# One core, a hybrid transformer block in split fp32r: a fourth Strassen pair in every FFN block, low halves of one K pair by ScalarE and an accumulating DMA, one Strassen pair fewer in the down projection, and the transposed mixer output in two tiles

## The chip, the core and the metric

The kernel runs on one core of a Trainium2 chip. The metric is the device time in microseconds (us) of one execution. TensorE (PE) multiplies, VectorE (DVE), ScalarE (ACT) and GpSimd (POOL) work beside it, and SyncE (SP) and POOL issue the DMAs.

## The reference, cut to what matters

The reference is one pre-norm block over 256 tokens of width 2048, in float32:

```
u = rms_norm(h, norm_mix)
z = u @ w_in                       # 2048 x 13060: inputs of four branches, 4*2048 merge gates
branches = (diff_attention, rg_lru, forgetting_attention, sliding_window_sink_attention)
gates = sigmoid(gz + b_gate)
mixed = sum(gates[n] * (branches[n] @ w_branch[n]) for n in range(4))
h = h + mixed @ w_out
v = rms_norm(h, norm_ffn)
h = h + (silu(v @ w_ffn_gate) * (v @ w_ffn_up)) @ w_ffn_down      # width 5632
out = rms_norm(h, norm_final)
```

## The kernel before

**Splitting.** PE multiplies in fp32r. So that nothing is lost, every fp32 operand is the sum of a high part (the value rounded to fp32r) and a low part (the value less the high part), and every product is three matmuls: high by high, high by low, low by high. A weight piece comes by DMA from SP into a tile `raw` (128 x 1024, two blocks of 128 rows); `wpiece` (L118) makes the high part `whi` by a copy on ACT and the low part `wlo` by a subtraction on DVE. `raw`, `whi` and `wlo` have four buffers each, which the pieces take in turn.

**Pairs.** `pair` (L245) computes two products of 512 columns side by side, a left and a right weight, for both halves t of the tokens (128 each) and both column halves i. It walks K in steps of 256 rows, called K pairs, numbered kp. An ordinary kp takes two pieces (left, right) and 2 x 2 x 2 x 3 = 24 matmuls into the accumulators `q[t][i]`. A Strassen kp (one in `skps`) goes by seven products in place of eight, so 21 matmuls; `s_weights` (L220) prepares it: two DMAs into `sx`, four DVE additions into `sx` and `se`, two ACT copies to the high parts `sh` (128 x 2048) and `seh` (128 x 1536), and two DVE subtractions to the low parts `sl` and `sel`. In the FFN and the down projection `sx`, `sh`, `sl`, `seh`, `sel` have two buffers, `se` has one. Four of the seven products gather in banks p1, p5, p6, p7, which DVE adds up in a tile `u` when the last Strassen kp is done. The last kp's products are held back to the end (`split`).

**Stages.** First come the branches, and then four gated chunks by `chunk` (L140), up to about 384 us. Six gated pairs follow to about 705 us (L803), each with a gate pair over eight kp and a branch pair over two. Their sums `mixed_of[c]` are four tiles of 512 columns. The first two are complete early: `nat_out` (L312) transposes them on PE and POOL writes them to four DRAM tiles `mrg`, at about 500 us. Then comes the output projection (L870), two pairs over eight kp with the transposed `mixed` as left operand, in one tile for the high and one for the low parts, `mth` and `mtl`. Its K blocks 0 to 7 come back from `mrg` by four DMAs of SP (`mload`, in a buffer of pool `fp`) and are split by ACT and DVE (`m_split`, L853); its K blocks 8 to 15 are transposed straight from `mixed_of[2]` and `mixed_of[3]` (`to_T`). The FFN (L894) has eleven blocks f of 512 hidden columns, each one pair over eight kp: gate weight left, up weight right. Block 0 has no Strassen kp, odd blocks have kp 0, 2, 3 and 5, even blocks kp 0, 3 and 5. The down projection (L944) has two pairs (cc 0 and 1) over 22 kp, Strassen at kp 3, 6, 9, 12, 15 and 18. Its left operand, the hidden layer, comes from DRAM (`hid`) into slices of `fin`; ACT and DVE split it into `ah`, and a Strassen kp needs four more small additions and a split on it (`s_sums`, L199).

**Order.** The program is built by a scheduler that sets the order of the instructions on each engine by itself. On the chip each engine takes its instructions as they stand and waits for semaphores. What the scheduler made of the code is therefore shown below by the instructions as they stand, beside the diff.

Of the kernel before, what the change touches and what calls it, by code (L numbers as in the profile page):

```python
# [8 lines left out]
F32 = mybir.dt.float32  # L9
# [5 lines left out]
P = 128  # L15
# [14 lines left out]
def hybrid_block_kernel(  # L30
# [47 lines left out]
    def rd(t):  # L78
        return t.bitcast(F32)
# [35 lines left out]
        tt(o, acc, t, ALU.mult)  # L115


    def wpiece(src, nk, n, pin=False):  # L118
        raw = wp.tile([P, nk, n], F32, tag="raw", name="raw", bufs=4)
        nc.sync.dma_start(raw, src.rearrange("(k p) n -> p k n", p=P))  # L120
        hi = wp.tile([P, nk, n], F32R, tag="whi", name="whi")
        lo = wp.tile([P, nk, n], F32R, tag="wlo", name="wlo")
        ins = (act(hi, raw), tt(lo, raw, rd(hi), ALU.subtract))
        if pin:
            for i in ins:
                tc.keep_in_program_order(i)
        return hi, lo
# [114 lines left out]
        while later:  # L242
            later.pop(0)()

    def pair(wl, wr, nkp, skps, a_of, upool=None, split=0, small_banks=False, at_mid=None):  # L245

# [22 lines left out]
        for kp in range(nkp):  # L271
# [3 lines left out]
            if kp in skps:  # L275
# [8 lines left out]
                if kp == skps[-1]:  # L284
# [8 lines left out]
                    run_later()  # L293
                continue
            rows = slice(kp * 2 * P, (kp + 1) * 2 * P)
            ws = [wpiece(w[rows, :], 2, 512) for w in (wl, wr)]
            todo = [((t, i), [(blk(j, t), (ws[i][0][:, j, :], ws[i][1][:, j, :])) for j in range(2)])
                    for t in range(2) for i in range(2)]
            if kp >= nkp - split:
                held.append(todo)  # L300
                continue
# [501 lines left out]
    for n, cc in ((2, 0), (0, 0), (1, 1), (3, 1), (2, 1), (0, 1)):  # L803
# [1 line left out]
        bb = mp.tile([P, 1024], F32, tag="bb2", name="bb2")  # L805
        nc.gpsimd.dma_start(bb, b_gate[0, col:col + 1024].partition_broadcast(P))
        col += C_GZ
        q, gate = pair(w_in[:, col:col + 512], w_in[:, col + 512:col + 1024], NKT // 2, GS, u_of, mp)
        for t in range(2):
            g = gate[:, 2 * t:2 * t + 2, :]  # L810
            tt(g, g, q[t], ALU.add)
# [27 lines left out]
    s3 = ExitStack()  # L839
    mxp = s3.enter_context(tc.tile_pool(name="mxp", bufs=1, side="right"))  # L840
    late["sx"] = mxp
    mth = mxp.tile([P, NKT, S], F32R, name="mth")
    mtl = mxp.tile([P, NKT, S], F32R, name="mtl")
    vth = uv.tile([P, NKT, S], F32R, tag="th", name="vth")
    vtl = uv.tile([P, NKT, S], F32R, tag="tl", name="vtl")
    ss2 = small.tile([P, 2, 2], F32, name="ss2", bufs=1)
    m_of = a_tiles(mth, mtl)


    for c in (2, 3):  # L850
        later.append(lambda c=c: to_T(mixed_of[c], mth, mtl, 4 * c))

    def m_split(kp, s):  # L853
        if kp > 3:
            return m_of(kp, s)
        if kp % 2 == 0:
            late["m"] = fp.tile([P, 2, 512], F32, tag="hd", name="mload")
        v = late["m"][:, kp % 2, :]
        nc.sync.dma_start(v, merged[kp])
        h, lo = (t[:, 2 * kp:2 * kp + 2, :].rearrange("p a b -> p (a b)") for t in (mth, mtl))  # L860
        act(h, v)
        tt(lo, v, rd(h), ALU.subtract)
        return m_of(kp, s)
# [29 lines left out]
    v_of = a_tiles(vth, vtl, FS, vsh, vsl)  # L893
    for f in range(DFF // 512):  # L894
        fs = slice(f * 512, (f + 1) * 512)
        q, u = pair(w_fg[:, fs], w_fu[:, fs], NKT // 2, () if f == 0 else FS if f % 2 else (0, 3, 5), v_of, fp, split=1)
        hd = fp.tile([P, 2, 512], F32, tag="hd", name="hd")

        if u is None:
            for t in range(2):  # L900
                act(hd[:, t, :], q[t][:, 0, :], AF.Silu, scale=rstd2[:, t:t + 1])
                tt(hd[:, t, :], hd[:, t, :], q[t][:, 1, :], ALU.mult)
        else:
            for t in range(2):
                o = u[:, 2 * t:2 * t + 2, :]
                tt(o, o, q[t], ALU.add)
                act(u[:, 2 * t, :], u[:, 2 * t, :], AF.Silu, scale=rstd2[:, t:t + 1])
            tt(hd, u[:, 0:4:2, :], u[:, 1:4:2, :], ALU.mult)
        later.append(lambda hd=hd, f=f: nat_out(hd, hid, f"hid{f}_"))
# [7 lines left out]
    nc.gpsimd.dma_start(gfin, norm_final.partition_broadcast(P))  # L917
    ss3 = small.tile([P, 2, 3], F32, name="ss3", bufs=1)
    ah = uv.tile([P, 4, 2, 2 * S], F32R, tag="tl", name="ah")
    DS = (3, 6, 9, 12, 15, 18)  # L920

    def h_of(cc, kp, with_sums):
        if cc == 0 and kp < 4:
# [91 lines left out]
```

## Time and profile before

| | |
|---|---|
| median of three runs | 1532.04 us (1528.97 to 1533.72) |
| the profiled execution | 1530.98 us, of it the span 1529.3 us |
| PE busy | 1497.3 us, 98% of the span |
| DVE, ACT, POOL busy | 78%, 53%, 5% |
| moved by DMA | 311.5 MB |

The span is the time from the first to the last instruction; 1.7 us of the profiled execution lie around it. The profile tells for each engine how long it was busy, and the trace gives every instruction with its start, its length and the idle time of the engine before it, with what ended this idle time. Matmuls overlap: each is listed with about 0.39 us, and the step from one start to the next is what it costs. The share of busy time is a mean over stages with different limits, so the stages are read one by one.

### The profile page before, as it was taken

What the parts mean: (1) busy time and instruction counts of PE and PEld (TensorE: products, weight loads), DVE (VectorE), ACT (ScalarE), POOL (GpSimd) and SP (SyncE); (2) the same over time, 40 slices, a digit from 0 to 9 for tenths busy, and PEclk for the clock granted to TensorE, in tenths of its full rate; (3) what the DMA queues carried; (4) which work ended last, traced back from release to release, by engine and by line L of the source; (5) the groups of instructions that cost most, each with busy time, mean ns of one, the idle gap of its engine ahead of it and who ended that gap; (6) DMA issues with size and microseconds to landing.
All of it is one profiled execution on the core that took longest, in us unless ns stands there. A gap on an engine that the chain in (4) does not pass through costs nothing.

```text
span 1529.3 us, 18519 instructions
## 1 busy us (share of the span) xinstructions
PE 1497.3 (98%) x6772; PEld 1230.8 (80%) x6772; DVE 1191.7 (78%) x1397; ACT 817.0 (53%) x944; POOL 74.4 (5%) x95
## 2 busy tenths in 40 slices
PE   8999999999999999998999999999999999999997
PEld 6878888888788888886888888888888888877875
DVE  4756745769779779866467899999999898899785
ACT  5545744545445544534356555555555565665553
POOL 4000300011100000000000000000000000001001
PEclk9999999999999999998999999999999999999999
DMA  7755465567566667565657666666756668776753
GB/s 231 214 146 166 136 182 153 170 186 247 179 207 218 222 207 218 181 192 193 192 178 237 220 220 221 203 234 205 233 176 233 191 223 302 241 235 215 237 178 125
DMA packets 158603, 311.54 MB, mean 204 GB/s; under 512 B 10608, under 2 KB 12720, under 8 KB 158384
## 3 DMA queue, kind: packets, MB, share of 16 engines
q1 hardware_dynamic: 154528, 297.87, 61.9%
q0 software_dynamic: 3952, 12.49, 2.6%
q8 instruction: 53, 0.87, 0.2%
q14 instruction: 38, 0.31, 0.1%
q10 hardware_dynamic: 32, 0.01, 0.0%
HBM read 301.41 MB, written 8.91 MB: 203 GB/s over the span
## 4 chain that ended last, share of the span: by engine, by line
PE 90%; DVE 4%; DMA 3%; issue 2%; ACT 0%; POOL 0%; SPq 0%; POOLq 0%; ACTq 0%; DVEq 0%
PE q L216 52%; PE acc L133 20%; PE p L216 14%; PE ps L165 2%; DMA fin<-hid 1%; DVE wlo L60 1%; DMA mload<-mrg 1%; DMA xq<-in_x_dram 1%; DVE sel L60 1%; DVE ah L60 0%; DVE se L60 0%; DMA raw<-in_w_in_dram 0%; PE ps L535 0%; PE ps L731 0%; PE ps L554 0%
## 5 line engine op out<-in xcount | busy, mean ns | idle before, releaser
L57 ACT ACTIVATE whi<-raw 128x1024 fp32r<-128x1024 f32 (+1 forms) x418 | 437.7, 1050 | 420.2 <-PE q L216 189.5
L60 DVE TENSOR_TENSOR wlo<-raw,whi 128x1024 fp32r<-128x1024 f32 (+1 forms) x418 | 509.0, 1224 | 190.4 <-ACT whi L57 187.5
L57 ACT ACTIVATE sh<-sx 128x2048 fp32r<-128x2048 f32 x59 | 113.0, 1916 | 120.7 <-issue 38.5
L133 PE MATMUL acc<-wlo,uth 128*128 128x512 f32 (+1 forms) x448 | 173.9, 391 | 0.0
L133 PE MATMUL acc<-whi,utl 128*128 128x512 f32 (+1 forms) x448 | 173.7, 389 | 0.0
L60 DVE TENSOR_TENSOR sl<-sx,sh 128x2048 fp32r<-128x2048 f32 x59 | 135.1, 2289 | 44.3 <-ACT sh L57 44.2
L133 PE MATMUL acc<-whi,uth 128*128 128x512 f32 (+1 forms) x448 | 167.9, 391 | 0.6 <-DVE nat L64 0.4
L216 PE MATMUL q<-wlo,vth 128*128 128x512 f32 x424 | 165.8, 391 | 0.0
L216 PE MATMUL q<-whi,vtl 128*128 128x512 f32 x424 | 165.6, 391 | 0.0
L216 PE MATMUL q<-whi,vth 128*128 128x512 f32 x424 | 164.5, 391 | 0.0
L216 PE MATMUL q<-whi,ah 128*128 128x512 f32 x480 | 151.4, 392 | 0.0
L216 PE MATMUL q<-whi,uth 128*128 128x512 f32 x288 | 111.0, 391 | 2.4 <-DVE gate L60 2.4
L216 PE MATMUL q<-wlo,uth 128*128 128x512 f32 x288 | 111.6, 390 | 0.0
L216 PE MATMUL q<-whi,utl 128*128 128x512 f32 x288 | 111.5, 390 | 0.0
L216 PEld LDWEIGHTS q<-whi,ah 128*128 128x128 f32 x480 | 90.8, 189 | 18.9
L60 DVE TENSOR_TENSOR sel<-se,seh 128x1536 fp32r<-128x1536 f32 x59 | 103.3, 1751 | 2.3 <-ACT seh L57 2.3
L216 PE MATMUL q<-wlo,ah 128*128 128x512 f32 x240 | 94.9, 395 | 4.9 <-DVE wlo L60 4.8
L133 PEld LDWEIGHTS acc<-wlo,uth 128*128 128x128 f32 x448 | 84.8, 189 | 17.0 <-issue 1.0
L133 PEld LDWEIGHTS acc<-whi,utl 128*128 128x128 f32 x448 | 84.8, 189 | 16.4 <-issue 0.7
L133 PEld LDWEIGHTS acc<-whi,uth 128*128 128x128 f32 x448 | 82.1, 189 | 16.9 <-issue 0.7
L57 ACT ACTIVATE seh<-se 128x1536 fp32r<-128x1536 f32 x59 | 87.2, 1479 | 15.7 <-DVE se L60 8.5
L216 PEld LDWEIGHTS q<-whi,vth 128*128 128x128 f32 x424 | 79.6, 188 | 16.3
(388 smaller groups left out, 2520.5 us busy)
## 6 DMA issues: line engine op xcount, KB each, us to landing
raw<-in_w_in_dram SPq DMA_DIRECT2D x168, 512.0 KB, 3.7
raw<-in_w_ffn_down_dram SPq DMA_DIRECT2D x64, 512.0 KB, 5.2
raw<-in_w_ffn_gate_dram SPq DMA_DIRECT2D x53, 512.0 KB, 4.2
raw<-in_w_ffn_up_dram SPq DMA_DIRECT2D x53, 512.0 KB, 4.8
sx<-in_w_ffn_up_dram SPq DMA_DIRECT2D x35, 512.0 KB, 3.8
sx<-in_w_ffn_gate_dram SPq DMA_DIRECT2D x35, 512.0 KB, 4.8
raw<-in_w_branch_dram SPq DMA_DIRECT2D x32, 512.0 KB, 4.4
raw<-in_w_out_dram SPq DMA_DIRECT2D x32, 512.0 KB, 4.5
```

Of the source, the lines that this page charges most:

```text
L57: return nc.scalar.activation(o, i, f, **kw)
L60: return (eng or nc.vector).tensor_tensor(out=o, in0=a, in1=b, op=op)
L133: m = nc.tensor.matmul(acc, x_, w_, start=st, stop=sp_)
L165: nc.tensor.transpose(pt[:, i * S + t * P:i * S + (t + 1) * P], nat[:, t, (c0 + i) * P:(c0 + i + 1) * P], ident)
L216: m = nc.tensor.matmul(acc, x_, w_, start=st, stop=sp_)
```

## The change

Five edits. (1) In `pair`, `swap` lets kp 0 begin with the token half t = 1; it is set for the first of the six gated pairs. (2) `mth` and `mtl` become two tiles each, one for K blocks 0 to 7 (`mh0`, `ml0`) and one for K blocks 8 to 15 (`mh1`, `ml1`), and `mload` takes the buffer `gate` of pool `gp`. (3) In FFN blocks 1 to 10 both pieces of kp 6 get their low part in another way: ACT writes the negated, rounded weight into `wlo`, and POOL issues a DMA that adds the weight from DRAM onto it; ACT makes `whi` as before. (4) FFN blocks 2, 4, 6, 8 and 10 get the fourth Strassen kp, 2. (5) In the down projection kp 18 becomes an ordinary one in both pairs.

```
-    def wpiece(src, nk, n, pin=False):
+    def wpiece(src, nk, n, pin=False, by_dma=False):
         raw = wp.tile([P, nk, n], F32, tag="raw", name="raw", bufs=4)
         nc.sync.dma_start(raw, src.rearrange("(k p) n -> p k n", p=P))
         hi = wp.tile([P, nk, n], F32R, tag="whi", name="whi")
         lo = wp.tile([P, nk, n], F32R, tag="wlo", name="wlo")
+        if by_dma:
+            act(lo, raw, scale=-1.0)
+            nc.gpsimd.dma_start(lo, src.rearrange("(k p) n -> p k n", p=P), accum_op=ALU.add)
+            act(hi, raw)
+            return hi, lo
...
-            ws = [wpiece(w[rows, :], 2, 512) for w in (wl, wr)]
+            ws = [wpiece(w[rows, :], 2, 512, by_dma=kp in dma_kps) for w in (wl, wr)]
             todo = [((t, i), [(blk(j, t), (ws[i][0][:, j, :], ws[i][1][:, j, :])) for j in range(2)])
-                    for t in range(2) for i in range(2)]
+                    for t in ((1, 0) if swap and kp == 0 else (0, 1)) for i in range(2)]
...
-        q, gate = pair(w_in[:, col:col + 512], w_in[:, col + 512:col + 1024], NKT // 2, GS, u_of, mp)
+        q, gate = pair(w_in[:, col:col + 512], w_in[:, col + 512:col + 1024], NKT // 2, GS, u_of, mp,
+                       swap=(n, cc) == (2, 0))
...
-    mth = mxp.tile([P, NKT, S], F32R, name="mth")
-    mtl = mxp.tile([P, NKT, S], F32R, name="mtl")
+    mt = [[mxp.tile([P, NKT // 2, S], F32R, name=f"m{hl}{half}") for hl in "hl"] for half in (1, 0)][::-1]
...
-    m_of = a_tiles(mth, mtl)
+    def m_of(kp, s):
+        return a_tiles(*mt[kp // 4])(kp % 4, s)
...
-        later.append(lambda c=c: to_T(mixed_of[c], mth, mtl, 4 * c))
+        later.append(lambda c=c: to_T(mixed_of[c], mt[1][0], mt[1][1], 4 * (c - 2)))
...
-            late["m"] = fp.tile([P, 2, 512], F32, tag="hd", name="mload")
+            late["m"] = gp.tile([P, 2, 512], F32, tag="gate", name="mload")
         v = late["m"][:, kp % 2, :]
         nc.sync.dma_start(v, merged[kp])
-        h, lo = (t[:, 2 * kp:2 * kp + 2, :].rearrange("p a b -> p (a b)") for t in (mth, mtl))
+        h, lo = (t[:, 2 * kp:2 * kp + 2, :].rearrange("p a b -> p (a b)") for t in mt[0])
...
-        q, u = pair(w_fg[:, fs], w_fu[:, fs], NKT // 2, () if f == 0 else FS if f % 2 else (0, 3, 5), v_of, fp, split=1)
+        q, u = pair(w_fg[:, fs], w_fu[:, fs], NKT // 2, () if f == 0 else FS, v_of, fp, split=1,
+                    dma_kps=() if f == 0 else (6,))
...
-    DS = (3, 6, 9, 12, 15, 18)
+    DS = (3, 6, 9, 12, 15)
```

The scheduler builds another order from this. ACT in FFN block 5, before: `sh_8244` and `seh_8246` are kp 3's, `whi_8373` and `whi_8379` kp 6's, `sh_8317` and `seh_8319` kp 5's, and `u` is the block before's.

```order
L57 ACTIVATE u_8025<-u_8025,rstd2_6471 128x512 x2
L57 ACTIVATE sh_8244<-sx_8240 128x2048
L57 ACTIVATE seh_8246<-se_8243 128x1536
L57 ACTIVATE whi_8373<-raw_8371 128x1024
L57 ACTIVATE whi_8379<-raw_8377 128x1024
L57 ACTIVATE sh_8317<-sx_8313 128x2048
L57 ACTIVATE seh_8319<-se_8316 128x1536
```

The same engine and block now: `seh_8221` is kp 2's, `wlo_8386` to `whi_8392` are kp 6's four, `sh_8256` and `seh_8258` kp 3's, `sh_8329` kp 5's.

```order
L57 ACTIVATE sh_8219<-sx_8215 128x2048
L57 ACTIVATE u_8035<-u_8035,rstd2_6473 128x512
L57 ACTIVATE seh_8221<-se_8218 128x1536
L57 ACTIVATE wlo_8386<-raw_8383 128x1024
L57 ACTIVATE whi_8385<-raw_8383 128x1024
L57 ACTIVATE wlo_8393<-raw_8390 128x1024
L57 ACTIVATE whi_8392<-raw_8390 128x1024
L57 ACTIVATE sh_8256<-sx_8252 128x2048
L57 ACTIVATE seh_8258<-se_8255 128x1536
L57 ACTIVATE sh_8329<-sx_8325 128x2048
```

Kp 6's copies stood behind kp 3's `sh` and `seh`; now there are four of them, and they stand ahead. Blocks 4, 8 and 9 have the order of block 5. In block 7 the fourth of them stands behind `sh`. In blocks 2 and 3, `sh` of kp 3 is still ahead of all four; block 1 keeps the old order. In block 6 (and so in block 10) two of the four stand even ahead of kp 2's `seh`, here `seh_8548`; kp 3's are `sh_8583` and `seh_8585`:

```order
L57 ACTIVATE sh_8546<-sx_8542 128x2048
L57 ACTIVATE u_8362<-u_8362,rstd2_6473 128x512
L57 ACTIVATE wlo_8713<-raw_8710 128x1024
L57 ACTIVATE whi_8712<-raw_8710 128x1024
L57 ACTIVATE seh_8548<-se_8545 128x1536
L57 ACTIVATE wlo_8720<-raw_8717 128x1024
L57 ACTIVATE whi_8719<-raw_8717 128x1024
L57 ACTIVATE sh_8583<-sx_8579 128x2048
L57 ACTIVATE seh_8585<-se_8582 128x1536
```

So kp 2's `seh`, and with it DVE's `sel` and the additions of kp 3 that reuse the one buffer `se`, come behind two of kp 6's copies. The second place is ACT at the start of the output projection, before (`ps` are banks with transposes by PE):

```order
L57 ACTIVATE mth_5765<-ps_5852 128x512
L57 ACTIVATE mth_5765<-ps_5859 128x512
L57 ACTIVATE mth_5765<-mload_5773 128x512
L57 ACTIVATE mth_5765<-ps_5866 128x512
L57 ACTIVATE mth_5765<-mload_5773 128x512
```

And now:

```order
L57 ACTIVATE mh0_5767<-mload_5775 128x512 x2
L57 ACTIVATE mh1_5765<-ps_5854 128x512
L57 ACTIVATE mh1_5765<-ps_5861 128x512
L57 ACTIVATE mh0_5767<-mload_5882 128x512 x2
L57 ACTIVATE mh1_5765<-ps_5868 128x512
```

The copies from `mload` moved ahead of those from the transposes. On SP the four `mload` DMAs moved from behind the loads of x and the first `w_out` pieces to a place some 70 instructions earlier, among the weight loads of the third gated pair; the fourth stands between the last two `w_in` pieces there:

```order
L120 DMA raw_4417<-in_w_in_dram 128x2x512
L868 DMA mload_5775<-mrg0_0_4194 128x512
L868 DMA mload_5775<-mrg0_1_4202 128x512
L868 DMA mload_5882<-mrg1_0_4210 128x512
L120 DMA raw_4447<-in_w_in_dram 128x2x512
L868 DMA mload_5882<-mrg1_1_4218 128x512
L120 DMA raw_4453<-in_w_in_dram 128x2x512
```

The third place is DVE in the down projection, cc 0. Before, behind kp 14's last `wlo` (`wlo_11233`), kp 18's sums (`fin`), `sl` and `sel` stood ahead of kp 16's first `wlo` (`wlo_11312`):

```order
L60 TENSOR_TENSOR wlo_11233<-raw_11230,whi_11232 128x1024
L60 TENSOR_TENSOR se_11396<-se_11396,sx_11393 128x512
L60 TENSOR_TENSOR fin_10076<-fin_10076 128x128 x4
L60 TENSOR_TENSOR sl_11398<-sx_11393,sh_11397 128x2048
L60 TENSOR_TENSOR ah_10079<-fin_10076,ah_10079 128x512
L60 TENSOR_TENSOR sel_11400<-se_11396,seh_11399 128x1536
L60 TENSOR_TENSOR vsl_5761<-fin_10076,vsh_5760 128x512
L60 TENSOR_TENSOR wlo_11312<-raw_11309,whi_11311 128x1024
```

Now the second pair's (cc 1) kp 3 stands there (`sl_11166`, `sel_11168`), and ahead of kp 18's first `wlo` (`wlo_10875`) stand the additions of `u`, cc 1's kp 6 (`sl_11294`, `sel_11296`) and the two updates of `hn`:

```order
L60 TENSOR_TENSOR wlo_10842<-raw_10839,whi_10841 128x1024
L60 TENSOR_TENSOR u_10784<-u_10784,p6_10275 128x512
L60 TENSOR_TENSOR u_10784<-u_10784,p7_10271 128x512
L60 TENSOR_TENSOR u_10784<-p5_10267,u_10784 128x2x512
L60 TENSOR_TENSOR sl_11294<-sx_11289,sh_11293 128x2048
L60 TENSOR_TENSOR ah_10106<-fin_10103,ah_10106 128x512
L68 SCALAR_TENSOR_TENSOR hn_5756<-u_10784,rstd2_6473,hn_5756 128x1024 x2
L60 TENSOR_TENSOR sel_11296<-se_11292,seh_11295 128x1536
L60 TENSOR_TENSOR wlo_10875<-raw_10872,whi_10874 128x1024
```

The `wlo` row at the top is kp 17's last; this group of `u`, kp 6 and `hn` stood ahead of kp 21's `wlo` before.

## Rows read from the trace of the kernel before

**Rows 1.** The page, busy us, share of the span, instructions.

```profile
PE 1497.3 (98%) x6772; PEld 1230.8 (80%) x6772; DVE 1191.7 (78%) x1397; ACT 817.0 (53%) x944; POOL 74.4 (5%) x95
```

**Rows 2.** The page, chain of work that ended last, shares by engine.

```profile
PE 90%; DVE 4%; DMA 3%; issue 2%; ACT 0%; POOL 0%; SPq 0%; POOLq 0%; ACTq 0%; DVEq 0%
```

**Rows 3.** Windows: stretch, length, busy PE, PEld, DVE, ACT, POOL, clock, DMA share, GB/s.

```profile
711.20:721.40 10.20, 6.81 (x19) 5.26 (x19) 3.84 (x7) 3.21 (x6) 0.00 (x0) 0.50 0.94 348
...
1023.64:1107.80 84.16, 84.16 (x380) 69.70 (x379) 78.24 (x74) 47.69 (x42) 2.76 (x4) 1.00 0.67 217
...
1360.00:1400.00 40.00, 35.93 (x149) 28.54 (x148) 39.90 (x43) 20.92 (x23) 0.00 (x0) 0.96 0.83 263
...
1393.60:1397.40 3.80, 3.80 (x11) 2.92 (x11) 3.80 (x6) 0.00 (x0) 0.00 (x0) 0.55 0.77 233
```

**Rows 4.** Timeline of PE, block 5, kp 1: start, length, instruction, idle before.

```profile
1032.71 0.39 PE L216 MATMUL q<-whi,vth 128*128 128x512 f32 x1
...
1034.52 0.39 PE L216 MATMUL q<-whi,vtl 128*128 128x512 f32 x1
...
1035.88 0.39 PE L216 MATMUL q<-whi,vtl 128*128 128x512 f32 x1
```

**Rows 5.** Timeline of ACT, block 5, kp 3, kp 6 and kp 5.

```profile
1030.19 1.92 ACT L57 ACTIVATE sh<-sx 128x2048 fp32r<-128x2048 f32 x1 [3.45 <-DVE se L60]
...
1035.00 1.06 ACT L57 ACTIVATE whi<-raw 128x1024 fp32r<-128x1024 f32 x1 [0.82 <-PE q L216]
1036.36 1.06 ACT L57 ACTIVATE whi<-raw 128x1024 fp32r<-128x1024 f32 x1 [0.30 <-PE q L216]
1039.74 1.92 ACT L57 ACTIVATE sh<-sx 128x2048 fp32r<-128x2048 f32 x1 [2.32 <-DVE sx L60]
1041.57 1.47 ACT L57 ACTIVATE seh<-se 128x1536 fp32r<-128x1536 f32 x1
```

**Rows 6.** Timeline of DVE, the same stretch.

```profile
1032.14 2.29 DVE L60 TENSOR_TENSOR sl<-sx,sh 128x2048 fp32r<-128x2048 f32 x1 [1.96 <-ACT sh L57]
1034.35 1.75 DVE L60 TENSOR_TENSOR sel<-se,seh 128x1536 fp32r<-128x1536 f32 x1
1036.10 1.23 DVE L60 TENSOR_TENSOR wlo<-raw,whi 128x1024 fp32r<-128x1024 f32 x1
...
1039.69 0.69 DVE L60 TENSOR_TENSOR se<-sx 128x512 f32<-128x512 f32 x1
1040.42 0.69 DVE L60 TENSOR_TENSOR se<-se,sx 128x512 f32<-128x512 f32 x1
```

**Rows 7.** Timeline of PE, first product of the first gated pair.

```profile
384.91 0.47 PE L216 MATMUL q<-whi,uth 128*128 128x512 f32 x1 [2.35 <-DVE gate L60]
```

**Rows 8.** Timeline of PE, then of ACT, start of the output projection.

```profile
711.32 1.54 PE L165 MATMUL ps<-ident,mixed 128*128 128x128 f32 x6 [1.41 <-DVE mixed L60]
716.13 0.79 PE L216 MATMUL q<-whi,mth 128*128 128x512 f32 x1 [3.27 <-ACT mth L57]
...
711.42 1.09 ACT L57 ACTIVATE mth<-ps 128x512 fp32r<-128x512 f32 x2 [3.26 <-DVE mixed L60]
715.45 0.63 ACT L57 ACTIVATE mth<-mload 128x512 fp32r<-128x512 f32 x1 [2.94 <-DMA mload<-mrg]
```

**Rows 9.** Timeline of POOL, the DMAs to `mrg`; then both tiles' DMA landing.

```profile
499.92 1.44 POOL L319 DMA_DIRECT2D mrg<-mixed  x2 [10.84 <-ACT mixed L57]
...
DMA to landing us min/median/max: 3.9/5.5/8.1
```

**Rows 10.** Timeline of PE, then of DVE, down projection, cc 0.

```profile
1362.27 0.50 PE L216 MATMUL q<-wlo,ah 128*128 128x512 f32 x1 [0.84 <-DVE wlo L60]
...
1392.62 0.50 PE L216 MATMUL q<-wlo,ah 128*128 128x512 f32 x1 [2.54 <-DVE wlo L60]
...
1354.99 1.02 DVE L60 TENSOR_TENSOR fin<-fin 128x128 f32<-128x128 f32 x4 [3.51 <-DMA fin<-hid]
...
1391.35 2.35 DVE L60 TENSOR_TENSOR wlo<-raw,whi 128x1024 fp32r<-128x1024 f32 x2
```

More of the change, by code (lines that the diff above doesn't have):

```diff
@@ L243, in run_later, with pair @@
             later.pop(0)()
-    def pair(wl, wr, nkp, skps, a_of, upool=None, split=0, small_banks=False, at_mid=None):
+    def pair(wl, wr, nkp, skps, a_of, upool=None, split=0, small_banks=False, at_mid=None, swap=False, dma_kps=()):
         pq = late["psum"]
```

## The prediction, made before the change was run

> **What bounds the kernel now.** I read the page first: PE is busy 98% of the span, and the chain of work that ended last lies 90% on PE [rows 1, 2]. So a change pays if it takes matmuls away or closes a gap of PE, and it costs if it opens one. Next I read the stages by windows. In two FFN blocks of 84.16 us PE is busy without a gap; DVE has 78.24 us of work there and ACT 47.69 [rows 3]. In the middle of the down projection PE has 35.93 of 40.00 us and DVE 39.90: there DVE is the bound [rows 3]. Then the gaps, in the timeline of PE. It waits 2.35 us for DVE's `gate` at the first gated pair [rows 7]; 3.27 us for ACT's copy of `mload` at the output projection [rows 8]; and 0.84 and 2.54 us for DVE's `wlo` in the down projection [rows 10]. Around two of these the granted clock is half, 0.50 and 0.55 in the windows [rows 3], and matmuls there cost twice. At full clock a matmul costs 0.226 us (14 steps from 1032.71 to 1035.88, [rows 4]).
>
> **Swap.** Kp 0 of the first gated pair begins with the other token half. In the built order its first product still waits for the same instruction of DVE, the last `gate`, since the accumulators take the place of the banks that it reads. The 2.35 us stay: 0. If the wait did go, 2.35 us would be the most.
>
> **Output projection.** Today ACT copies two transposes at 711.42 and then sits 2.94 us until `mload` lands; PE's first product starts at 716.13 [rows 8]. Now the four `mload` DMAs are issued in the third gated pair, right behind the `mrg` DMAs that they read. These are issued from 499.92 on and land in 3.9 to 8.1 us [rows 9], and SP waits for that. The two weight pieces queued behind are held back by 1 to 3 us, my estimate from these landings; the pieces run four buffers, two kp or 48 x 0.226 = 10.9 us of PE, ahead, so this is hidden, and would show once that lead is under 3 us. At 711 ACT then copies `mload` at once (0.63 us each), while PE still has its six transposes, until 711.32 + 1.54 = 712.86. The first product can start there: 716.13 - 712.86 = 3.3 us. The clock decides the rest. It is half until 721.4 [rows 3], so the 5.3 us from 716.13 on hold 2.6 us of loss. If the half clock goes on until 721.4 anyway, 8.5 us at half rate lose 4.3, and the gain is 1.6; if it ends soon after the earlier start, up to 5. I take -3.3, range -5 to -1.6.
>
> **FFN, matmuls.** Five blocks get 21 in place of 24 matmuls for kp 2: 15 x 0.226 = -3.4 us on PE. DVE pays for a Strassen pair four additions of 0.69, 2.29 and 1.75 [rows 6], 6.8 us in place of two `wlo` of 1.23; kp 6 gives two of these back in each block. For two blocks (one of them gets a Strassen pair more) that is 78.24 + 4.35 - 4.9 = 77.7 us of DVE against 83.5 of PE; ACT gets 47.69 + 4 x 1.06 + 1.3 = 53.2. Neither is full, so by the sums alone the gain holds.
>
> **FFN, order on ACT.** This is the term on which I decide. Kp 6's tiles reuse the buffers of kp 1, so ACT's first copy for kp 6 waits until PE is through with kp 1's left piece. Rows 4 and 5 show this wait: the matmul at 1034.52 releases `whi` at 1035.00, after 0.48 us, and the right piece follows six matmuls later. Today kp 3's `sh` is done by then, at 1030.19 + 1.92. In the new order `sh` stands behind the four copies of kp 6. Let t = 0 be the start of the releasing matmul. The copies start at 0.48 and take 1.06 less 0.09 each (the overlap of `sh` and `seh` at 1041.57, [rows 5]), so `sh` runs from 4.4 to 6.3, `seh` to 7.7, and DVE's `sl` from 6.3 to 8.6. PE has 7 matmuls of kp 1 and 21 of kp 2 left, 6.35 us, then reaches kp 3. In its order it can do three products with `sh`, must have `seh` for three, then `sl`: it waits about 0.65 and 0.3, 1.0 us in all. So in blocks 4, 5, 8 and 9: 4.0. Block 7, with three copies ahead: 0.8. In blocks 6 and 10 kp 2's `seh` runs only from 2.4 to 3.9, `sel` to 5.7, and PE, which needs it at 5.0, waits 0.8. Behind `sel` come kp 3's additions (one buffer `se`), so `sh` starts at 7.0 and ends at 8.9, `seh` at 10.3, `sl` at 11.3, where PE arrives at 7.15: waits of 1.85, 0.75 and 0.3. Together 3.7, twice 7.4. Sum +12.2 us; kp 5 is then no longer late. Bounds: 0, if PE is held up elsewhere and the lead comes back; about twice that if the clock falls too.
>
> **FFN, the accumulating DMA.** No row shows one. ACT's second low part ends at t = 3.4, POOL issues in 0.72 (1.44 for two) and a POOL DMA lands within 8.1 us [rows 9]: done at 12.2 at the latest. PE needs it at kp 6, 6.35 + 71 x 0.226 = 22.4. It is hidden with 10 us to spare: 0, and above zero only if it took more than twice the longest landing shown.
>
> **Down projection.** Kp 18 costs PE 3 x 0.226 = 0.7 in each pair. In cc 0 DVE waited 3.51 us for `hid` before kp 18's sums [rows 10]; with the sums (1.0), `sl`, `sel` and two small splits (0.6 each in steps) this is 9.8 us ahead of kp 16's `wlo`. In its place stand cc 1's `sl` and `sel` of kp 3 and two small ones, 5.2 us, so kp 16's `wlo` come over 4 us earlier and PE's wait there (0.84, and a second like it) closes. But then `u`, cc 1's kp 6 and `hn`, some 9.5 us that end at 1391.35 today, stand ahead of kp 18's `wlo`, not of kp 21's. From 1354.99 - 3.51 = 1351.5: 5.2, then 8.2 for kp 16 and 17 (four `wlo` at 1.14 in steps, six small ones), 9.5, and 1.2 for kp 18's first `wlo`, which ends at 1375.6. PE would need it 50 matmuls after 1362.27 - 0.84 - 0.39 = 1361.0, at 1372.4: a wait of 3.3 takes the place of the 2.54 at 1392.62. Behind it DVE is ahead: 94 matmuls from 1375.7 end cc 0 at 1397.0. Today 23 matmuls from 1392.62 and 1.7 us for the half clock there (3.8 us at 0.55, [rows 3]) make it 1399.5. That is -2.5, with cc 0's kp 18 in it. With +0.7 for cc 1's kp 18 and half a microsecond less waiting there: -2.3, range -5 to +2.
>
> **Sum.** The profiled run took 1530.98 us, of it 1529.3 in the span. 0 - 3.3 - 3.4 + 12.2 + 0 - 2.3 = +3.2, so 1534.2. The median of the runs lies 1.06 higher, and there I put the forecast: 1535.
>
> **The rivals.** (B) The FFN shows its matmul count and no new waits: -3.3 - 3.4 - 2.3 = -9, 1523. For it: ACT has 57% of work and DVE 93%, and today the low parts are 6 us ahead of PE at this place [rows 3 to 6]. The Trainium skill, Perfetto Trace Analysis, Optimizing Scalar/DVE Operations, says that moving work to Scalar can pay if DVE is saturated; by it the time would be this one. But the trace shows no wait of PE for DVE in the FFN, so there is no wait there for it to remove. Against B: the wait for kp 1 sets t = 0 anew in every block, and no lead gets past it on an engine that takes its instructions as they stand. (C) Slower: the waits of blocks 6 and 10 (3.7 us within some 7) and the one at kp 18 bring the clock down as the 2.54 at 1392.62 did; each costs 1.7 to 2.6 more. Two or three of them give +3.4 to +7.8: about 1540. It decides once one clock fall per long wait is added, since the sum then passes +4.6. Against it: the 2.35 us at 384.91 had no such fall. (D) Slower by far: POOL's accumulating DMA comes late at kp 6. Each us beyond the 10 us of slack counts ten times; 2 us over gives +20, 1555. The Trainium skill, GPSIMD Engine Reference, Key points, says that GpSimd shares its SBUF interfaces with VectorE and contends with instructions that have two SBUF inputs, as nearly all of DVE's here are; that would speak for D. But the POOL DMAs of [rows 9] were issued beside such work in 0.72 us each.
>
> **How the numbers follow.** A, the walk as it stands: 0.40, 1529 to 1538. B: 0.27, 1519 to 1528. C: 0.29, 1536 to 1545. D: 0.04. A run of this kernel tells 0.3%, 4.6 us, from no change: below 1527.4 is faster, above 1536.6 slower. Faster: B but for its edge, 0.25. Same: 0.32 of A and 0.02 each of B and C, 0.36. Slower: the rest of A and C, and D, 0.39. The range leaves out D, the best of B and the worst of C: 1520 to 1543; A's own is 1529 to 1538.
>
> **What would show it.** In the FFN, PE rows with idle time before `sh`, `seh` and `sl` of kp 3, ended by ACT and DVE, about 1 us in blocks 4, 5, 8, 9 and over 3 in 6 and 10, none in 1 to 3; ACT's row for kp 6's `wlo` with PE as releaser right before. The first product of the output projection near 713 less what came before. In the down projection one wait of about 3 us at kp 18 and none at kp 16 and 21. If PE is gapless in the FFN, B holds; if the clock row there is below 1.00, C.

## The result

The changed kernel takes 1538.79 us (median of six runs, 1536.19 to 1542.24) against 1531.01 us for the kernel before beside it: a ratio of 1.0052 with a 95% interval of 1.0038 to 1.0066. It is slower by 0.5%, and lies in the forecast range of 1520 to 1543, 3.8 us above the forecast of 1535. Its profiled execution took 1536.19 us with a span of 1534.5, which is 5.2 above the profiled execution before; it is the fastest of the six, and the medians lie 7.8 apart.

The page after, the busy times and the two DMA queues that carry the load (their packets, MB, share of the 16 engines' span):

```profile
PE 1499.6 (98%) x6763; PEld 1228.0 (80%) x6763; DVE 1183.1 (77%) x1379; ACT 840.6 (55%) x962; POOL 99.3 (6%) x115
...
q1 hardware_dynamic: 154528, 297.87, 60.3%
q0 software_dynamic: 9392, 22.97, 6.4%
```

PE still looks busy 98% [rows 1], so the page does not tell what happened. The first products of the stages do; the stretches between them are:

| stretch, by PE's first products | before | after | difference |
|---|---|---|---|
| start to the first gated pair | 384.91 | 382.88 | -2.0 |
| first gated pair to output projection | 331.22 | 327.17 | -4.1 |
| output projection to FFN block 0 | 93.81 | 92.92 | -0.9 |
| FFN block 0 to the down projection | 466.34 | 479.95 | +13.6 |
| down projection, first pair | 123.34 | 119.42 | -3.9 |
| second pair to the span's end | 129.7 | 132.2 | +2.5 |

Nothing is changed in the first stretch; the other kernels below begin this pair between 382 and 385 us, so its 2 us are scatter. The loss lies in the FFN and at its end: the +13.6 hold a wait of 4.8 us at the down projection's first product. (A number in the brackets of a row is idle time by the profile. Where the text gives a wait of PE without its row, it is the step from one matmul's start to the next, less the usual 0.23 us, and comes out some 0.15 us higher.) Windows over blocks 3 to 10 after, two blocks in each (columns as in [rows 3]); the last one ends with the wait just named:

```profile
934.99:1018.80 83.81, 83.66 (x376) 68.62 (x374) 74.79 (x71) 50.24 (x45) 7.83 (x8) 1.00 0.79 237
1018.80:1107.10 88.30, 85.73 (x380) 69.05 (x378) 79.36 (x75) 53.50 (x47) 7.81 (x8) 1.00 0.76 227
1107.10:1192.70 85.60, 84.10 (x376) 68.48 (x375) 76.27 (x73) 51.41 (x46) 7.89 (x8) 1.00 0.78 234
1192.70:1282.90 90.20, 82.89 (x365) 66.11 (x364) 77.05 (x73) 51.69 (x47) 8.37 (x9) 1.00 0.73 218
```

Before, two blocks took 84.16 us with PE busy in all of them. Now they take up to 90.2, PE's busy time falls short by up to 2.6 (in the last window by 7.3, 4.67 of it at the down projection's first product), and the clock stays whole. Where it waits is seen in the timeline of PE in block 6, kp 2 and kp 3:

```profile
1072.64 0.50 PE L221 MATMUL p<-sel,vsh 128*128 128x512 f32 x1 [0.28 <-DVE sel L60]
...
1076.03 0.50 PE L221 MATMUL p<-sh,vth 128*128 128x512 f32 x1 [1.72 <-ACT sh L57]
...
1077.41 0.73 PE L221 MATMUL p<-seh,vsh 128*128 128x512 f32 x2 [0.41 <-ACT seh L57]
...
1078.36 0.50 PE L221 MATMUL p<-sl,vth 128*128 128x512 f32 x1
```

and on ACT, which releases it, with the DVE row that waits for ACT (last):

```profile
1067.40 1.06 ACT L57 ACTIVATE wlo<-raw 128x1024 fp32r<-128x1024 f32 x1 [4.48 <-PE q L221]
1068.37 1.04 ACT L57 ACTIVATE whi<-raw 128x1024 fp32r<-128x1024 f32 x1
1069.32 1.47 ACT L57 ACTIVATE seh<-se 128x1536 fp32r<-128x1536 f32 x1
1070.69 1.04 ACT L57 ACTIVATE wlo<-raw 128x1024 fp32r<-128x1024 f32 x1
1071.64 1.04 ACT L57 ACTIVATE whi<-raw 128x1024 fp32r<-128x1024 f32 x1
1074.07 1.91 ACT L57 ACTIVATE sh<-sx 128x2048 fp32r<-128x2048 f32 x1 [1.39 <-DVE sx L60]
1075.88 1.47 ACT L57 ACTIVATE seh<-se 128x1536 fp32r<-128x1536 f32 x1
...
1070.82 1.76 DVE L60 TENSOR_TENSOR sel<-se,seh 128x1536 fp32r<-128x1536 f32 x1 [3.82 <-ACT seh L57]
```

ACT idles 4.48 us until PE releases kp 1's buffer, makes two copies for kp 6, and only then kp 2's `seh`, for which DVE has been waiting 3.82 us. This is the walk of the prediction nearly to the tenth: with its t = 0 at 1066.92 (the first copy's 1067.40 less the 0.48 of the walk), `seh` was to run from 2.4, `sh` from 7.0 and PE to arrive at 7.15; the rows give 2.4, 7.15 and 7.23.

A second loss was not on the list. The down projection's first product waits:

```profile
1282.92 0.47 PE L221 MATMUL q<-whi,vsh 128*128 128x512 f32 x1 [4.67 <-DVE u L60]
...
1280.95 0.69 DVE L60 TENSOR_TENSOR sx<-sx 128x512 f32<-128x512 f32 x1 [0.63 <-DMA sx<-in_w_ffn_down_dram]
1281.56 1.22 DVE L60 TENSOR_TENSOR u<-u,q 128x1024 f32<-128x1024 f32 x1
```

The first row is PE, the others DVE. PE's accumulators are those of FFN block 10, and the addition `u<-u,q` that empties them stands on DVE behind additions for the down projection that wait for their weights. These waits are short, 0.53 and 0.63 us; for the rest of PE's 4.67 DVE is at work on what stands ahead, because it comes late to this place. One of the earlier waits that made it late has these rows: the issue of block 10's last accumulating DMA by POOL, the last use of `sx` by block 10 on DVE, the issue of the down projection's first load into `sx` by SP, and DVE's wait for that load.

```profile
1245.87 1.23 POOL L125 DMA_DIRECT2D wlo<-in_w_ffn_up_dram  x1 [2.04 <-ACT wlo L57]
...
1260.02 2.29 DVE L60 TENSOR_TENSOR sl<-sx,sh 128x2048 fp32r<-128x2048 f32 x1
...
1262.34 0.38 SPq L229 DMA_DIRECT2D sx<-in_w_ffn_down_dram  x1
...
1266.68 0.69 DVE L60 TENSOR_TENSOR se<-sx 128x512 f32<-128x512 f32 x1 [1.56 <-DMA sx<-in_w_ffn_down_dram]
```

The load is issued when DVE has made kp 5's `sl` (1260.02 + 2.29), 15.5 us ahead of PE's last product of the FFN; before, it was issued at 1247.36, over 28 us ahead. It and the load right behind it land in 4.2 and 5.2 us (before, in 4.5 and 5.5), and block 10's accumulating DMAs had both landed by 1256.2, six us before it was issued. The half clock follows PE's wait, as it does behind a like wait at the second down pair (windows):

```profile
1283.50:1287.00 3.50, 3.50 (x10) 2.79 (x9) 3.50 (x7) 2.69 (x5) 0.00 (x0) 0.53 1.01 399
1409.50:1413.00 3.50, 3.50 (x10) 2.69 (x10) 3.50 (x3) 1.99 (x3) 2.48 (x1) 0.53 0.52 169
```

### The profile page after: what moved, and what is told of

Same layout as the page of the kernel before. It is cut to its first block, busy times and chain, and to the rows that moved or that the text cites. A ratio compares the mean times of both kernels' runs of the same rounds, so it can differ in the third digit from the quotient of the medians.

```text
span 1534.5 us, 18550 instructions
## 1 busy us (share of the span) xinstructions
PE 1499.6 (98%) x6763; PEld 1228.0 (80%) x6763; DVE 1183.1 (77%) x1379; ACT 840.6 (55%) x962; POOL 99.3 (6%) x115
## 3 DMA queue, kind: packets, MB, share of 16 engines
q1 hardware_dynamic: 154528, 297.87, 60.3%
q0 software_dynamic: 9392, 22.97, 6.4%
## 5 line engine op out<-in xcount | busy, mean ns | idle before, releaser
L57 ACT ACTIVATE whi<-raw 128x1024 fp32r<-128x1024 f32 (+1 forms) x412 | 431.9, 1050 | 416.2 <-PE q L221 209.7
L60 DVE TENSOR_TENSOR wlo<-raw,whi 128x1024 fp32r<-128x1024 f32 (+1 forms) x392 | 478.9, 1226 | 205.1 <-ACT whi L57 201.7
L60 DVE TENSOR_TENSOR sl<-sx,sh 128x2048 fp32r<-128x2048 f32 x62 | 141.9, 2289 | 45.5 <-ACT sh L57 45.4
L57 ACT ACTIVATE sh<-sx 128x2048 fp32r<-128x2048 f32 x62 | 118.7, 1914 | 103.3 <-issue 39.3
L221 PE MATMUL q<-whi,ah 128*128 128x512 f32 x512 | 161.0, 392 | 2.6 <-DVE hn L68 2.5
L221 PE MATMUL q<-whi,vtl 128*128 128x512 f32 x384 | 150.1, 391 | 0.0
L221 PE MATMUL q<-whi,vth 128*128 128x512 f32 x384 | 149.9, 392 | 0.0
L221 PE MATMUL q<-wlo,vth 128*128 128x512 f32 x384 | 149.4, 390 | 0.0
L221 PEld LDWEIGHTS q<-whi,ah 128*128 128x128 f32 x512 | 96.9, 189 | 23.6 <-DVE hn L68 3.0
L60 DVE TENSOR_TENSOR se<-sx 128x512 f32<-128x512 f32 x124 | 85.4, 689 | 11.6 <-DMA sx<-in_w_in_dram 7.6
```

Source lines behind the costliest of these rows:

```text
L57: return nc.scalar.activation(o, i, f, **kw)
L60: return (eng or nc.vector).tensor_tensor(out=o, in0=a, in1=b, op=op)
L221: m = nc.tensor.matmul(acc, x_, w_, start=st, stop=sp_)
```

## The experiments

All ratios are to the kernel before. "The changed kernel" stands for its code, with the edit named.

**The order on ACT.** One constraint is added: ACT takes kp 6's four copies behind kp 3's `seh` of the same block.

```
-        act(eh, e)
+        m = act(eh, e)
+        if kp == 3:
+            late["seh3"] = m.ins
...
+  # each of act(lo, raw, scale=-1.0) and act(hi, raw) in wpiece, as m:
+            tc.add_manual_dep(m.ins, late["seh3"].name, <order only, no wait>)
```

> The changed kernel with one more constraint: in every FFN block ACT takes kp 6's four copies only behind kp 3's seh. Theory (kp 6's copies hold kp 3's sh back): PE's waits in blocks 4 to 10, 9.5 us in the trace of the changed kernel, shrink to 2 or less, so about 1531 us (-7.5 from 1538.8); the wait at the start of the down projection stays. Rival (VectorE itself has no time left with four Strassen pairs in each block, and the order on ACT only shows it): most of the waits stay, over 5 us, and the time is 1535 or more.

Measured: 1530.1 us, ratio 1.0000 (0.9988 to 1.0012), so 8.7 below the changed kernel (8 by the two ratios). In blocks 4 and 5 the waits are gone, in 7 and 9 all but 0.16 us; blocks 6, 8 and 10 keep about 1 us each, and in block 8 that is more than the 0.5 it had. Block 6, PE and ACT, then DVE in block 6 and in block 7:

```profile
1073.31 0.50 PE L223 MATMUL p<-sh,vth 128*128 128x512 f32 x1 [0.20 <-ACT sh L57]
...
1074.68 0.50 PE L223 MATMUL p<-seh,vsh 128*128 128x512 f32 x1 [0.40 <-ACT seh L57]
...
1071.34 1.92 ACT L57 ACTIVATE sh<-sx 128x2048 fp32r<-128x2048 f32 x1 [3.40 <-DVE sx L60]
...
1064.60 1.22 DVE L60 TENSOR_TENSOR hd<-u 128x1024 f32<-128x1024 f32 x1
1065.73 0.68 DVE L60 TENSOR_TENSOR se<-se,sx 128x512 f32<-128x512 f32 x1
1067.97 1.76 DVE L60 TENSOR_TENSOR sel<-se,seh 128x1536 fp32r<-128x1536 f32 x1 [1.56 <-ACT seh L57]
...
1107.81 0.69 DVE L60 TENSOR_TENSOR se<-se,sx 128x512 f32<-128x512 f32 x1
1108.41 1.22 DVE L60 TENSOR_TENSOR hd<-u 128x1024 f32<-128x1024 f32 x1
1110.05 1.76 DVE L60 TENSOR_TENSOR sel<-se,seh 128x1536 fp32r<-128x1536 f32 x1 [0.42 <-ACT seh L57]
```

Now ACT waits for DVE, 3.40 us, so what is left comes from VectorE. But it is not shown to be a lack of time there. In blocks 6, 8 and 10 `hd` stands ahead of kp 2's last addition into `se`, ACT therefore makes `seh` later, and VectorE itself idles 1.56 us for it. In blocks 7 and 9 the addition stands ahead of `hd`, VectorE idles 0.42 us, and PE waits 0.16. So the theory holds for most of the loss; the rest, which the rival puts down to a full VectorE, goes with an order again, that on VectorE. To change that order, or to give `se` a second buffer, was not tried. The wait at the down projection's start stays (4.7 us).

**The four pairs without the DMA.** First kp 6's low parts go back to VectorE (`dma_kps=()`), then the same with ACT's order mended.

> The changed kernel without the accumulating DMA: four Strassen pairs in blocks 1 to 10, kp 6's low parts by VectorE. VectorE then has 41.6 us of work in each block against 40.8 of PE. Theory (VectorE is the limit and the DMA is what makes room): PE waits of 8 to 12 us over the blocks from the third or fourth on, 1530 to 1536 us. Rival (VectorE has time enough, and the DMA gives nothing): 1522 to 1526.

> Four Strassen pairs in blocks 1 to 10, no accumulating DMA, and kp 6's copies on ACT behind kp 3's seh as in the run with the order mended. Theory (VectorE has 41.6 us of work in a block against 40.8 of PE, so it is the limit without the DMA): PE waits of about 1 us in each block from the third or fourth on, 7 to 10 in all, 1533 to 1537 us. Rival (only the order mattered): 1530 or less, as with the DMA.

Measured: 1542.54 us, ratio 1.0081 (1.0054 to 1.0107), and 1540.32, ratio 1.0064 (1.0044 to 1.0085). Both lie above the ranges of their theories. Each is slower than the version with the DMA in the same order (1538.8 and 1530.1), though for the first of the two the intervals overlap. A window of 166 us in the FFN of the second (columns as in [rows 3]), and then its timeline of PE in block 6:

```profile
934.00:1100.00 166.00, 161.75 (x715) 130.45 (x714) 155.65 (x146) 92.07 (x80) 4.61 (x7) 1.00 0.62 203
```

```profile
1079.55 0.50 PE L222 MATMUL p<-sh,vth 128*128 128x512 f32 x1 [1.36 <-ACT sh L57]
```

Waits at kp 3 of 0.7 to 2.4 us stand in every block from block 3 on. Between order_mended and four_order only the DMA differs, with the order that the scheduler builds from it: 1530.1 against 1540.3. So the DMA does what it is there for: without it, with four pairs in each block, VectorE is busy 155.65 of 166 us, 94%, and PE waits for what it makes. The Trainium skill says in Perfetto Trace Analysis, Optimizing Scalar/DVE Operations, that moving work to Scalar may make sense if DVE is saturated; the 10 us agree with it here.

**The FFN as before, and the DMA alone.** In the one, `pair` gets the old sets and no DMA; in the other the old sets and the DMA for kp 6.

```
-  NKT // 2, () if f == 0 else FS, v_of, fp, split=1, dma_kps=() if f == 0 else (6,))
+  NKT // 2, () if f == 0 else FS if f % 2 else (0, 3, 5), v_of, fp, split=1)               # ffn_as_before
+  NKT // 2, () if f == 0 else FS if f % 2 else (0, 3, 5), v_of, fp, split=1,
+                                                          dma_kps=() if f == 0 else (6,))  # dma_only
```

> The changed kernel with the FFN as it was (three and four Strassen pairs in turn, no accumulating DMA); the two tiles for the transposed mixer output, the swap and the down projection's edit stay. Theory: the output projection keeps its gain (-4.9 by the two traces), the down projection gains 2 more by the walk of the prediction: 1524 us (-7 from 1531.0). Rival (the early gain is given back further on): 1529 to 1532.

> The changed kernel with the accumulating DMA for kp 6 in blocks 1 to 10, but three and four Strassen pairs in turn as before. Here kp 6's copies stand behind kp 3's sh. Theory (the accumulating DMA itself costs nothing, its landing of 7.4 to 11.6 us is hidden): within 1 us of the run with the FFN as before, about 1524. Rival (its traffic or POOL's work slows VectorE or the loads): 3 us or more above that run, with PE waits in the FFN.

Measured: 1525.57 us, ratio 0.9964 (0.9952 to 0.9977), and 1528.32, ratio 0.9989 (0.9973 to 1.0004). The first shows PE gapless through the FFN, and in the down projection the wait at kp 18 that the prediction had walked to 3.3 us, and one for `hn` at the second pair:

```profile
1368.96 0.60 PE L221 MATMUL q<-wlo,ah 128*128 128x512 f32 x1 [2.28 <-DVE wlo L60]
...
1399.00 0.50 PE L221 MATMUL q<-whi,ah 128*128 128x512 f32 x1 [2.54 <-DVE hn L68]
```

The second is gapless in the FFN too, as its theory has it, but it is 2.7 us above the first: PE waits 5.4 us at the down projection's first product. VectorE there in the timeline, and then, from the view of the tile `sx`, how long its loads took (min, median, max):

```profile
1259.71 0.69 DVE L60 TENSOR_TENSOR se<-sx 128x512 f32<-128x512 f32 x1 [4.56 <-DMA sx<-in_w_ffn_down_dram]
```

```profile
DMA to landing us min/median/max: 4.1/5.5/10.7
```

**What makes PE wait at the down projection's start.** Three tries. Block 10 of the changed kernel gets three pairs:

> The changed kernel with three Strassen pairs (kp 0, 3, 5) in FFN block 10 alone. Theory (the fourth pair of the last FFN block takes a buffer sx that the down projection's first Strassen weights need, so their load comes late, VectorE waits for it and PE waits for VectorE): the gap of 4.8 us at the first product of the down projection and its half clock (2 us) go, as do block 10's own waits (3 us), for 0.7 us more matmuls: -9, some of it given back at kp 18 of the down projection where VectorE then has less lead (up to +3.3): 1530 to 1533 us. Rival (the load is late through the accumulating DMAs' traffic): the gap stays, and only block 10's waits go: about 1536.

Measured: 1541.7 us, ratio 1.0077 (1.0051 to 1.0104). The theory falls as it stands: the gap is not gone but 6.0 us, a wait of 2.2 us at kp 18 comes in, and a second stall of 1.6 stands before the one at the second pair. But the run does not clear the fourth pair. Its load into `sx` is issued at 1257.52, while block 10's accumulating DMAs are still on their way (until 1263.5), and lands in 7.2 and 8.0 us, and VectorE waits 5.62 us for it, so one cause came in as another went. Next, on top of ACT's order, the additions for the down projection's kp 6 are put behind block 10's `u<-u,q`:

> The run with ACT's order mended, and one more constraint: on VectorE the additions for kp 6 of the down projection's first pair stand behind the two additions by which FFN block 10 empties its accumulators. Theory (the first product of the down projection waits only because the emptying of the accumulators stands behind additions that wait for a load): its gap of 4.7 us and the half clock behind (about 2) go; at kp 18, where VectorE then has less lead, up to 3 us come back: 1524 to 1528 us against 1530.1. Rival (the late load itself holds PE, whatever the order): the gap stays, about 1530.

Measured: 1530.31 us, ratio 0.9992 (0.9981 to 1.0004), no change against order_mended. The gap is 4.1 us: kp 3's additions, which wait 4.07 us for their load, stand ahead now. Here and in order_mended, too, this load is issued among the accumulating DMAs; in order_mended it lands in 8.2 and 9.2 us. Mending one place in the queue moved the wait to the next. Then the DMA is left out in block 10 alone, with the old sets:

```
-                    dma_kps=() if f == 0 else (6,))
+                    dma_kps=() if f in (0, 10) else (6,))
```

> The run with the accumulating DMA and three and four pairs in turn, but without the accumulating DMA in FFN block 10. With it the weights of the down projection's first Strassen pairs took 9.8 us to land, VectorE waited 4.6 us for them and PE 5.4 at the down projection's first product; without any accumulating DMA they landed in 4.2 and PE did not wait. Theory (block 10's accumulating DMAs, which land in 10 us at the same time, slow that load): the load lands in 4 to 6 us, the gap goes, 1523 to 1525 us against 1528.3. Rival (the gap comes from the order that the scheduler chose): it stays, 1527 or more.

Measured: 1522.36 us, ratio 0.9947 (0.9928 to 0.9966). The timeline of PE at the down projection's start and of VectorE's wait, and then the loads into `sx` by the view of the tile:

```profile
1270.68 0.47 PE L221 MATMUL q<-whi,vsh 128*128 128x512 f32 x1 [0.29 <-DVE u L60]
...
1256.98 0.69 DVE L60 TENSOR_TENSOR se<-sx 128x512 f32<-128x512 f32 x1 [0.79 <-DMA sx<-in_w_ffn_down_dram]
```

```profile
DMA to landing us min/median/max: 4.1/5.0/6.1
```

Against dma_only the order on VectorE at this place is nearly the same, the longest landing falls from 10.7 to 6.1 us, VectorE's wait from 4.56 to 0.79 and PE's from 5.4 to 0.45. So in that kernel it was block 10's accumulating DMAs that slowed the weights' load: it was issued at 1249.83, and the last of them landed at 1257.7. In the changed kernel it was not, for there the load is issued six us after they have landed and lands in 4.2 and 5.2 us. There VectorE comes late to the end of block 10, behind the waits on ACT in that block, and the load starts only when kp 5's `sl` is done. The two kernels without any accumulating DMA but with four pairs (above) have waits of 2.3 and 2.9 us at this place, so VectorE's lateness alone is enough for a wait. That the late load and the order on VectorE make up the whole 4.8 us of the changed kernel is read from its trace; no run takes them away.

**The down projection.** First the kernel before with edits (1) and (2) alone; then the FFN as before with the down projection's edit and two constraints on VectorE: the second pair's sums behind the updates of `hn` that empty the accumulators, and the second pair's kp 6 behind the first pair's last `wlo`.

```
+   # first addition of s_sums, as m, once the first pair's last update of hn is traced
+   tc.add_manual_dep(m.ins, late["hn_done"].name, <order only>)
+   # first addition of s_weights for cc 1, kp 6, as m
+   tc.add_manual_dep(m.ins, late["lo"].name, <order only>)
```

> The kernel before with two edits alone, the two tiles for the transposed mixer output and the swap; FFN and down projection as before. Theory: the output projection gains 4.9 and nothing is given back, 1526 us; against the run that has the down projection's edit too (1525.6) this says what that edit is worth: 0 to 2 us. Rival: over 1528, the down projection's edit carries part of the gain.

> The run with the FFN as before, with the same two constraints in the down projection. Its trace has waits of 2.4 us at kp 18 and 2.7 at the second pair's start with half clock behind both. Theory: these go, 1525.6 - 5 to 8 = 1518 to 1521 us. Rival (VectorE late in the second pair): 1524 or more.

Measured: 1525.86 us, ratio 0.9971 (0.9961 to 0.9980), and 1521.6 us, ratio 0.9940 (0.9924 to 0.9956). So the two tiles for the transposed mixer output are the gain of ffn_as_before (1525.57), and leaving kp 18 out is worth nothing by itself. With the order mended 4 us more are gained; whether the two constraints would bring as much with kp 18 left a Strassen pair was not tried. Kp 18's wait is gone, and at the second pair PE now waits 0.16 us for `hn`, though 1.99 us for a hidden tile a little later:

```profile
1388.84 0.47 PE L225 MATMUL q<-whi,ah 128*128 128x512 f32 x1 [0.16 <-DVE hn L68]
...
1394.06 0.69 PE L225 MATMUL p<-sh,ah 128*128 128x512 f32 x1 [1.99 <-ACT ah L57]
```

**All of it together.** The four pairs with every constraint so far, and then with block 10 on three pairs and without its DMA (there without the constraint at the down projection's start).

> The run before with two more constraints on VectorE: the updates of hn that empty the first down pair's accumulators stand ahead of the second pair's sums, and the second pair's kp 6 is prepared behind the first pair's last wlo. Theory: the waits at kp 18 and at the second pair's start (2.7 us each and their half clock) go too, 1519 to 1522 us. Rival (VectorE has no time in the second pair for the work moved there): new waits there, 1524 or more.

> Four Strassen pairs and the accumulating DMA with ACT's order mended in blocks 1 to 9, block 10 with three pairs and no such DMA, and the two constraints in the down projection. Against 1521.6 us for the FFN as before with these constraints: theory (four pairs save 0.68 us in each of four even blocks and lose about 1 us in blocks 6 and 8): 1520 to 1522 us, no gain that can be told. Rival (with the last block free of the DMA the four pairs pay in full): 1518.5 or less; other rival (VectorE reaches the down projection without its lead): 1525 or more.

Measured: 1527.78 us, ratio 0.9986 (0.9973 to 0.9998), and 1526.58, ratio 0.9979 (0.9965 to 0.9993). In the first the waits at kp 18 and for `hn` go, but the start keeps 4.2 us and 2.2 us of waiting for a hidden tile come new. In the second the start keeps 1.3 us, and 3 us come new at the first Strassen pair, beside 2.4 for a hidden tile:

```profile
1287.01 0.50 PE L227 MATMUL p<-sh,vsh 128*128 128x512 f32 x1 [2.96 <-ACT hd L57]
```

Neither reaches the 1521.6 us of the version with the old FFN, which is the fastest that was run and beats both kernels: 0.6% below the kernel before. The DMA in blocks 1 to 9 with the old sets (1522.36) cannot be told from it and needs no constraint; both together were not tried.

## Why the prediction was right, and where it was not

The mechanism on which the prediction decided, the order on ACT in the FFN, is the one that occurred. That the time came out so near has luck in it. Of the +5.2 between the two profiled executions, the FFN up to its last product has +8.8, which is the forecast's -3.4 + 12.2; the wait at the down projection's start adds 4.8, for which the prediction had no term, and -2.0 of scatter in the first stretch and 1.6 more gain at the output projection than forecast cover most of it. By the medians the change is +7.8.

**Swap.** 0, as forecast: the first product still waits 2.35 us for the last `gate`, in every kernel run.

```profile
382.88 0.47 PE L221 MATMUL q<-whi,uth 128*128 128x512 f32 x1 [2.35 <-DVE gate L60]
```

**Output projection.** Forecast -3.3 in -5 to -1.6, measured -4.9. The mechanism was right, the clock went the better way:

```profile
709.30 0.96 PE L170 MATMUL ps<-ident,mixed 128*128 128x128 f32 x6 [1.41 <-DVE mixed L60]
710.05 0.77 PE L221 MATMUL q<-whi,mh 128*128 128x512 f32 x1
...
713.18 0.49 PE L221 MATMUL q<-whi,ml 128*128 128x512 f32 x1
...
709.32 1.15 ACT L57 ACTIVATE mh<-mload 128x512 fp32r<-128x512 f32 x2 [3.19 <-DVE mixed L60]
```

ACT copies `mload` at once (last row), PE goes from the transposes to the products without a wait [rows 8 had 3.27], and steps of 0.43 us end at 713.2, 3.9 us after the last wait, where before they ran on to 721.4.

**FFN, matmuls.** 2088 matmuls in place of 2103 between the first products of the FFN and of the down projection: -3.4, as forecast.

**FFN, order on ACT.** Forecast +12.2. All waits and restarts of PE in the FFN sum to 11.8 us more than before (the gap at the down projection's start left out). By blocks, the long steps cost 0.5 in blocks 4, 5, 8 and 9 (forecast 1.0), 1.5 in block 7 (0.8) and 3.1 in 6 and 10 (3.7), and each restart some tenths. So the long steps come to 9.5, less than the walk's 12.2, and some 2 us of restarts, which it did not have, fill the difference: the waits stand where they were forecast, but the agreement of the sums is partly chance. The cause was also named too narrowly. The walk took the order on ACT as the reason; order_mended shows that some 7 of the 11.8 are its doing. The rest goes with VectorE, which the prediction had dismissed with "neither is full"; at kp 2 and kp 3, where two Strassen pairs follow each other with one buffer `se`, ACT and VectorE wait for each other in turn, whatever their sums.

**FFN, accumulating DMA.** Forecast 0, hidden. At kp 6 that is right, although both bounds were too low:

```profile
L125 POOL DMA_DIRECT2D wlo<-in_w_ffn_gate_dram x10: 1234/1243/1271, 862.2 to 1242.6; - x10
...
DMA to landing us min/median/max: 7.4/9.5/11.6
```

POOL needs 1.24 us (0.72 assumed) and the landing up to 11.6 (8.1). The 10 us of slack covered it. What the term left out is whose load this DMA slows. In dma_only that cost 5 us at the down projection's start; in the changed kernel itself no load of the down projection's Strassen weights was in flight beside block 10's, so there the term's 0 stands.

**Down projection.** Forecast -2.3, measured -3.9 in the first pair, and +2.5 in the second with the tail, so -1.4 together (a half clock that costs 1.6 at its start is within the -3.9). But the wait of 4.8 us at its start costs more than that. This is the step that failed: the prediction walked the down projection from the old trace's times and put the change from the FFN to it at nothing, without a reason, while VectorE, held up in block 10, came to it late. Kp 18's wait of 3.3 was right for the kernel with the old FFN (2.3) and absent in the changed one, since PE's stall at the start gave VectorE a lead. The second pair's wait for `hn` was not foreseen; there VectorE's row tells a story of its own:

```profile
1405.54 2.46 DVE L60 TENSOR_TENSOR fin<-fin 128x128 f32<-128x128 f32 x1
1407.92 1.27 DVE L68 SCALAR_TENSOR_TENSOR hn<-q,rstd,hn 128x1024 f32<-128x1024 f32 x1
...
1405.48 2.36 POOL L60 TENSOR_TENSOR hn<-hn,fin 128x1024 f32<-128x1024 f32 x1 [105.49 <-ACT junk L57]
```

A small addition that takes 0.28 us elsewhere lasts 2.46 while POOL's multiplication (last row) runs, and `hn`, for which PE waits, stands behind it.

**The rivals.** A, the walk, was the case in its mechanism, but the time of 1538.8 lies just above A's own range of 1529 to 1538, by the wait at the down projection's start, and above the 1536.6 from which the prediction calls a kernel slower; to that it gave 0.39. C gave the nearest number, 1540, by a mechanism that did not occur: the clock is 1.00 through the FFN. It falls twice, in the down projection, behind waits that the prediction did not have. B is refuted by the changed kernel itself and, in a way, by order_mended: even with the order mended the four pairs give back what they save. D did not occur: no matmul waits at kp 6. Its argument from VectorE's two inputs does not show in the trace either: the eight `sel` that overlap POOL's issue of an accumulating DMA took at most 1.76 us, as long as the others (1.75).

## What to carry to other kernels

An instruction that waits for a buffer holds back everything behind it on its engine, so a copy for a later step must not stand ahead of one that is needed sooner; walk the first repeating block with the durations of the old trace before trusting a saving in matmuls. If a mean says that an engine has a few per cent left, look at the place where its work comes in a row, and at the end of a stage, where an engine that is late carries its lateness into the next. Ask of an added DMA not only who waits for it, but also whose load lands at the same time.

## What the runs showed of the hardware

- The accumulating DMAs were slow, and they slowed loads that were in flight beside them. Queue q0 moved 12.49 MB in 2.6% of the engines' span before and 22.97 MB in 6.4% after, so 0.36% for each of the 10.48 MB added, against 60.3 / 297.87 = 0.20% on q1 and 0.21% on q0 itself before. In dma_only two plain loads of 512 KB beside them took 9.8 and 10.7 us; in dma_not_in_10 the same two took 4.9 and 5.8. The Trainium skill, DMA: Bandwidth & Descriptors, Rules for kernel authors, says that an accumulate reads its destination and writes it later, which fits the cost, but no run here separates the read.
- A VectorE addition of 128 x 128 took 2.46 us beside a POOL multiplication of 2.36, and 0.28 without. This agrees with the sharing that the Trainium skill, GPSIMD Engine Reference, Key points, states; beside POOL's issue of accumulating DMAs, to which the prediction tied it, VectorE's times are the usual ones (above). Why that issue takes POOL 1.24 us and not 0.72 stays open.
- The clock fell to half after waits of 4.67 and 2.54 us of PE and not in block 6, where 0.28, 1.72 and 0.41 us came within 5 us. The length of one wait does not decide alone: behind the same wait of 2.35 us at the first gated pair the clock stayed at 1.00 in the changed kernel (window 382.9 to 390) and was 0.72 in all_mended (384 to 390), and it fell after 1.99 us in ffn_before_down_mended but not after 2.24 in four_pairs_to_9.
